# A hybrid decoder step on one core: sample readouts moved among the z tiles, gate squares summed on VectorE before one ones product, low parts of z and output weights made by adding DMAs

## The chip, the core and the metric

The kernel runs on one core of one Trainium2 chip. The core has a matrix engine (TensorE, "PE" in the profile, with "PEld" for its weight loads), a vector engine (VectorE, "DVE"), a scalar engine (ScalarE, "ACT"), GpSimd ("POOL") and SyncE ("SP"). Each engine runs its own instructions in order, and waits for others by semaphores. Here SP issues nearly all plain loads and stores, and POOL issues the DMAs that add into their destination. The metric is the device time of one execution in microseconds; the median of several runs counts.

## What is computed

One step of a decoder trunk for 512 prompt positions and 8 sample tokens, 520 columns in all, with features on the 128 partitions. A SwiGLU feed-forward block is followed by a mixer (a pooling branch and a state-space branch with a gate) and a second feed-forward block. The change lies in the mixer:

```python
def _hybrid_mixer(h, ...):
    proj = h @ w_in
    u_pool, z, xbc, dt_raw = jnp.split(proj, ...)
    pool_out, new_pool = _pool_mix(u_pool, ...)
    xbc_act, new_conv = _causal_conv(xbc, ...)
    ...
    y, h_new = _ssd_scan(xs_h, dt, A, B, C, ssm_h0, chunk)
    y = y + d_skip[:, None] * xs_h
    y = y.reshape(b, T, SSD_DIM) * jax.nn.silu(z)
    yg = y.reshape(b, T, SSD_GROUPS, SSD_DIM // SSD_GROUPS)
    yg = yg * lax.rsqrt(jnp.mean(yg * yg, axis=-1, keepdims=True) + EPS)
    y = yg.reshape(b, T, SSD_DIM) * ssd_norm
    cat = jnp.concatenate([pool_out, y], axis=-1)
    return cat @ w_out, new_pool, new_conv, h_new
```

## The kernel before

**Products in three parts.** TensorE multiplies fp32r numbers. To keep fp32 precision, weights and activations are split into a high part (rounded to fp32r) and a low part (what is left). `mm3` issues high x high (L123), high x low (L126) and low x high (L127) into one PSUM bank. A weight unit is 128 x 1024 fp32, 512 KB. `load_unit` has SP load it into a half of a raw tile (two pairs, four halves), and `split` makes the parts: ScalarE copies the high part (L107), VectorE subtracts it from the raw weights to get the low part (L114). `split` can also make the low part in another way, which the feed-forward blocks use for half of their units: ScalarE writes the negated weights, rounded to fp32r, into the low tile (L110), and POOL issues a DMA that reads the weights from HBM and adds them to it (L111). High and low tiles have three buffers each (`whi`, `wlo`), which all units of the mixer go through in the order of their use: a unit's tiles come free when TensorE is done with the unit three places before it.

**The mixer's stages.** Two strings, `CONV_PLAN` and `GATE_PLAN`, and a third, `LAST_PLAN`, set the order in which the program is written; a scheduler then orders the instructions of each engine by its own model of time. In the strings, `b` and `x` are convolution tiles, `p` pooling tiles, `z0` to `z7` the eight gate tiles (`zproj`: one weight unit, two halves of 260 columns in two PSUM banks, then VectorE multiplies by the norm into `zs`, L1113). `A` and `B` are the two parts of a chunk of the state-space scan, four chunks by two groups: `ssd_a` makes the decay tile `ab` (loaded by SP from a scratch in HBM, L1048) and `ssd_b` multiplies on TensorE (`yo`, `pst`, `yd`, L1083 to L1089). `s2` is two of the 16 sample readouts: SP loads a row `cb` (three buffers) and a state tile `h` (four buffers), and VectorE makes four products with an accumulated sum each (L975). `G` is the gate of a group (`gate`: silu of `zs`, product with X, L1139), and `H` its norm (`gate_out`). `o`, `g` and `h` are the 12 output weight units, four each of the pooling part and the two gate groups (`wout`: TensorE, then VectorE adds to the residual `h`, L1123). `n` fills the second feed-forward block's first products.

**The norm of a gate group** (`gate_out`, called by `H0` and `H1`). ScalarE squares four tiles of 128 x 520 (L1145). `rstd` sums them over the partitions with a product by a 128 x 128 tile of ones in plain fp32, four tiles accumulated into one bank, for each of the two halves (L170, tile `psr_y`): eight products for a group. ScalarE takes the root (L171), VectorE the reciprocal (L172), multiplies `zs` by it (L1152), ScalarE writes the high part `catg` (L1153), VectorE the low one (L1154), and the units `g` or `h` read them.

**PSUM.** The mixer has eight banks in rotation; a product's bank is the one used eight allocations earlier, and is free when that one has been read.

Of the kernel before, what the change touches and what calls it, by code (L numbers as in the profile page):

```python
# [12 lines left out]
ALU = mybir.AluOpType  # L13
# [4 lines left out]
D = 1024  # L18
# [21 lines left out]
    "c3 X1 m2 A3 B2 e0"  # L40
)
GATE_PLAN = (
    "A4 z0 B3 z1 m3 z2 B4 z3 s2 A5 z4 s2 B5 A6 z5 s2 s2 G0 z6 A7 z7 B6 s2 o0 H0 s2 o1 B7 s2 o2 s2 G1 "
    "o3 g0 g1 H1 g2 g3"
)
LAST_PLAN = "h0 h2 h1 n0 h3 n1 n2 n3"
# [15 lines left out]
def tile_trunk_step(ctx: ExitStack, tc: tile.TileContext, ins: dict, outs: dict):  # L62
    nc = tc.nc
# [6 lines left out]
    wp = ctx.enter_context(tc.tile_pool(name="wp", bufs=3, side="right"))  # L70
# [25 lines left out]
    def raw_tile(name):  # L96
        if not half:
            t = raw_pair(name)
            half.extend([t[:, 1], t[:, 0]])
        return half.pop()  # L100

    def split(src, n, name, hp, nb, tags, late=None):
        hi, lo = (hp.tile([P, 1024], F32R, tag=t, bufs=nb, name=f"{t}_{name}")[:, :n] for t in tags)
        h, l = hi, lo
        if len(src.shape) == 3:
            h, l = (t.rearrange("p (j c) -> p j c", j=src.shape[1]) for t in (hi, lo))
        nc.scalar.copy(h, src)  # L107
        q = 0 if late is None else n - late.shape[1]
        if late is not None:
            nc.scalar.activation(out=lo[:, q:], in_=src[:, q:], func=AF.Copy, scale=-1.0)  # L110
            nc.gpsimd.dma_start(out=lo[:, q:], in_=late, accum_op=ALU.add)  # L111
        if late is None or q:
            s = slice(0, q) if late is not None else slice(None)
            nc.vector.tensor_tensor(out=l[:, s], in0=src[:, s], in1=h[:, s].bitcast(F32), op=ALU.subtract)  # L114
        return hi, lo

    def load_unit(src, n, name):
        raw = raw_tile(name)[:, :n]
        nc.sync.dma_start(out=raw, in_=src)
        return split(raw, n, name, wp, 3, ("whi", "wlo"))  # L120

    def mm3(ps, whi, wlo, xhi, xlo, start, stop, pin=False, **kw):
        first = nc.tensor.matmul(ps, whi, xhi, start=start, stop=False, **kw)  # L123
# [84 lines left out]
    class Ffn:  # L208
# [310 lines left out]
        def down(self, c, lo, hi, after):  # L519
            n = hi - lo  # L520
            banks, units = {}, {}

            def part(d, ks):
                if d not in units:
                    units[d] = load_unit(ins[f"w{self.i}d"][d, :, lo * P : hi * P], n * P, f"{self.i}d{d}_{c}")
                    banks[d] = ps[0].tile([P, 2, 512], F32, tag="BE", bufs=2, name=f"dn{self.i}_{d}_{c}")
                wh, wl = units[d]
                for b in range(2):
                    for k in ks:
                        g = self.g[lo + k]  # L530
                        mm3(banks[d][:, b, :HB], ws(wh, k), ws(wl, k), g[:, 0, b], g[:, 1, b], k == 0, k == n - 1)

            def done(d):
                for b, hs in enumerate(HALVES):
                    nc.vector.tensor_tensor(out=h[:, d, hs], in0=banks[d][:, b, :HB], in1=h[:, d, hs], op=ALU.add)
                    after(d, b, hs)

            part(0, range(n - 1))
            part(1, range(n - 1))
            part(0, range(n - 1, n))  # L540
            done(0)
            part(1, range(n - 1, n))
            done(1)
            for d in range(2, KD):
                part(d, range(n))
                done(d)
# [54 lines left out]
    for j in range(KD // 2):  # L601
        for d in (j, j + KD // 2):
            q = slice(NVEC + d * NT if d else 0, NVEC + (d + 1) * NT)
# [87 lines left out]
    todo, late = [], []  # L691
# [48 lines left out]
def mixer(tc, ins, outs, e):  # L740
    nc = tc.nc
    cst, act, wp, tmp, dr, pool = (e[x] for x in ("cst", "act", "wp", "tmp", "dr", "pool"))
    ones = e["ones"]
    bank, load_unit, mm3, ws, v, rstd, rstds, vec, h, nx2, raw_tile, open_f2, fin, fill = (
        e[x] for x in ("bank", "load_unit", "mm3", "ws", "v", "rstd", "rstds", "vec", "h", "nx2", "raw_tile",
                       "open_f2", "fin", "fill"))
# [19 lines left out]
    X = mp.tile([P, NX, NT], F32, tag="X", name="X")  # L766
# [1 line left out]
    npp = mp.tile([P, 4, PAST], F32, tag="npp", name="npp")  # L768
    ncp = mp.tile([P, 12, 3], F32, tag="ncp", name="ncp")

    def inproj(src, name):
        wh, wl = load_unit(src, D, f"in{name}")
        bs = [bank(f"in{name}{b}") for b in range(2)]
        for b, hs in enumerate(HALVES):
            for k in range(KD):
                mm3(bs[b][:, :HB], ws(wh, k), ws(wl, k), xh[:, k, hs], xl[:, k, hs], k == 0, k == KD - 1)
        return bs
# [111 lines left out]
    def pooling(g):  # L889
        w = WINDOWS[g]  # L890
        bs = inproj(ins["w_in"][12 + g], f"p{g}")
        U = cv[0].tile([P, LP], F32, tag="cu", bufs=6, name=f"PU{g}")
        us = U[:, SAMPLE_P:LP].rearrange("p (b j) -> p b j", j=16)
# [214 lines left out]
    def zproj(j):  # L1108
        if not zbox:
            zbox.append(cv[0].tile([P, NX, NT], F32, tag="zs", name="zs"))  # L1110
        bs = inproj(ins["w_in"][16 + j], f"z{j}")
        for b, hs in enumerate(HALVES):
            nc.vector.tensor_tensor(out=zbox[0][:, j, hs], in0=bs[b][:, :HB], in1=r[:, hs], op=ALU.mult)  # L1113

    def wout(cat, j, d2, fin=None):
        wh, wl = load_unit(ins["w_out"][j, d2], 1024, f"wo{j}{d2}")
        for d in (2 * d2, 2 * d2 + 1):
            for b, hs in enumerate(HALVES):
                ps = bank(f"wo{j}_{d}{b}")
                for k in range(4):  # L1120
                    i = (d % 2) * 4 + k
                    mm3(ps[:, :HB], ws(wh, i), ws(wl, i), cat[:, 0, k, hs], cat[:, 1, k, hs], k == 0, k == 3)
                nc.vector.tensor_tensor(out=h[:, d, hs], in0=ps[:, :HB], in1=h[:, d, hs], op=ALU.add)  # L1123
                if fin is not None:
                    fin(d, b, hs)
# [15 lines left out]
    def gate_out(g):  # L1141
        zs = zbox[0]
        ry = mp.tile([P, NT], F32, tag="wph", name=f"yr{g}")
        for q in range(4):
            nc.scalar.activation(out=X[:, 4 * g + q], in_=zs[:, 4 * g + q], func=AF.Square)  # L1145
        for b, hs in enumerate(HALVES):
            rstd(ry, [X[:, 4 * g + q, hs] for q in range(4)], hs, 512, f"y{g}{b}")
        cat = cats[g] = xa.tile([P, 2, 4, NT], F32R, tag="xa", bufs=2, name=f"catg{g}")
        for q in range(4):
            i = 4 * g + q  # L1150
            gn = v("ssd_norm", i)
            nc.vector.tensor_tensor(out=zs[:, i], in0=zs[:, i], in1=ry, op=ALU.mult)  # L1152
            nc.scalar.activation(out=cat[:, 0, q], in_=zs[:, i], func=AF.Copy, scale=gn)  # L1153
            nc.vector.scalar_tensor_tensor(out=cat[:, 1, q], in0=zs[:, i], scalar=gn, in1=cat[:, 0, q].bitcast(F32),  # L1154
                                           op0=ALU.mult, op1=ALU.subtract)
# [13 lines left out]
    def outs_a():  # L1169
# [4 lines left out]

    stages = {
        "b": lambda j: conv(8 + j, inproj(ins["w_in"][j], f"bc{j}"), BC[:, j]),
        "x": lambda j: conv(j, inproj(ins["w_in"][4 + j], f"x{j}"), X[:, j]),
        "d": lambda j: box.update(dta=token_dt()) if j == 0 else (token_acs(box["dta"]), sample_decay()) if j == 1 else head_acs(),
# [7 lines left out]
        "A": lambda j: ssd_a(*ssd(j)),  # L1186
        "B": lambda j: ssd_b(*ssd(j)),
        "z": zproj,
        "o": lambda j: wout(catp, 0, j),
        "G": gate,  # L1190
        "H": gate_out,
        "g": lambda j: wout(cats[0], 1, j),
        "h": lambda j: wout(cats[1], 2, j, fin),
        "n": fill,
        "e": lambda j: outs_a(),
# [101 lines left out]
```

## Time and profile before

The median of three runs is 982.45 us. The execution that was profiled took 982.63 us, and its span on the core is 980.9 us, 1.7 us less. All times of the trace are microseconds from the start of that span.

| what | value |
|---|---|
| runs | 980.93, 982.45, 982.63 us |
| profiled execution, and its span | 982.63 us, 980.9 us |
| z tiles on TensorE | 472.9 to 532 us |
| output units on TensorE | 534.6 to 628 us |
| ScalarE busy from 445 to 605 us | 76.9 of 160 us |
| VectorE busy from 445 to 605 us | 141.5 of 160 us |
| GpSimd busy from 445 to 605 us | 37.1 of 160 us |

In the profile, a group's row gives its line, engine, operation, output and inputs, count, busy time, mean time of one, and the idle time of the engine just before it with what ended it. A window's row gives busy times by engine, the granted TensorE clock as a share of full speed, and the DMA engines' share.

### The profile page before, as it was taken

The numbers are of one execution on the slowest core, as the hardware profiler recorded it, in microseconds if no ns is written. First come the engines' busy times: TensorE is split into PE (matmuls) and PEld (weight loads), VectorE is DVE, ScalarE is ACT, GpSimd is POOL, SyncE is SP. The second block draws the span as 40 slices with busy tenths as digits, with TensorE's granted clock in tenths as the row PEclk, the third lists the DMA queues.
The fourth block names the chain that finished last, engine by engine and source line by source line (L and its number), as shares of the span: only waits on it lengthen the run. The fifth ranks groups of instructions, "written<-read, shape, count | busy, mean of one in ns | idle before, by whom it ended". The sixth has DMA issues, their size and how long they took to land.

```text
span 980.9 us, 20300 instructions
## 1 busy us (share of the span) xinstructions
PE 950.7 (97%) x7660; PEld 928.2 (95%) x7660; DVE 876.8 (89%) x1624; ACT 682.9 (70%) x1267; POOL 220.3 (22%) x321
## 2 busy tenths in 40 slices
PE   7999999999999999999999999999999999999996
PEld 6999999999999999999899998899999999999995
DVE  7999899989988698688979987999999998999976
ACT  8777777777777565694754335678888888887864
POOL 0111211221121000167311000113343233233300
PEclk9999999999999999999999999999999999999998
DMA  7666766576566242363334333357687768767732
GB/s 244 179 145 141 184 141 161 128 183 165 120 158 162 78 159 87 103 210 92 120 98 164 100 110 94 106 149 165 165 215 184 183 157 223 191 155 190 190 91 88
DMA packets 63858, 146.51 MB, mean 149 GB/s; under 512 B 9288, under 2 KB 22536, under 8 KB 63760
## 3 DMA queue, kind: packets, MB, share of 16 engines
q1 hardware_dynamic: 41168, 103.78, 33.3%
q0 software_dynamic: 22592, 41.43, 23.3%
q8 instruction: 60, 0.98, 0.4%
q14 instruction: 38, 0.31, 0.1%
HBM read 137.85 MB, written 7.34 MB: 148 GB/s over the span
## 4 chain that ended last, share of the span: by engine, by line
PE 82%; DVE 9%; ACT 3%; DMA 3%; issue 2%; SPq 0%; POOL 0%; DVEq 0%; ACTq 0%
PE A L127 7%; PE A L123 7%; PE A L126 7%; PE BE L123 6%; PE BE L126 6%; PE BE L127 6%; PE P L315 3%; PE wo L123 2%; PE wo L127 2%; PE wo L126 2%; PE inz L123 2%; PE inz L126 2%; PE inz L127 2%; PE A2d L126 2%; PE A2d L127 2%
## 5 line engine op out<-in xcount | busy, mean ns | idle before, releaser
L437 ACT COPY ac<-A 128x260 f32<-128x260 f32 x123 | 45.3, 370 | 19.5 <-PE A L127 19.2
L385 DVE TENSOR_TENSOR s<-raw 128x1024 f32<-128x1024 f32 x41 | 49.9, 1217 | 2.0 <-DMA raw<-in_w2gu 0.9
L107 ACT CAST whi_wo<-raw_wo 128x1024 fp32r<-128x1024 f32 x12 | 12.6, 1046 | 36.8 <-issue 10.3
L1005 POOL DMA_DIRECT2D out_nss<-hs x32 | 20.8, 649 | 76.8 <-DVE hs L1023 76.8
L126 PE MATMUL wo<-catg,whi_wo 128*128 128x260 f32 x128 | 36.4, 285 | 1.3 <-DVE catg L1154 1.3
L123 PE MATMUL wo<-catg,whi_wo 128*128 128x260 f32 x128 | 37.3, 292 | 0.3 <-DVE h L1123 0.3
L123 PE MATMUL inz<-xh_mx,whi_inz 128*128 128x260 f32 x128 | 37.5, 293 | 0.0
L315 PE MATMUL P<-xg_f,raw 128*128 128x260 f32 x128 | 31.7, 401 | 5.5 <-ACT sq_f L163 5.5
L126 PE MATMUL inz<-xl_mx,whi_inz 128*128 128x260 f32 x128 | 36.9, 288 | 0.0
L127 PE MATMUL inz<-xh_mx,wlo_inz 128*128 128x260 f32 x128 | 36.9, 288 | 0.0
L123 PE MATMUL inx<-xh_mx,whi_inx 128*128 128x260 f32 x128 | 36.4, 285 | 0.0
L127 PE MATMUL wo<-catg,wlo_wo 128*128 128x260 f32 x128 | 36.4, 285 | 0.0
L127 PE MATMUL inx<-xh_mx,wlo_inx 128*128 128x260 f32 x128 | 36.2, 283 | 0.0
L126 PE MATMUL inx<-xl_mx,whi_inx 128*128 128x260 f32 x128 | 36.1, 282 | 0.0
L315 PEld LDWEIGHTS P<-xg_f,raw 128*128 128x128 f32 x128 | 25.2, 201 | 9.3 <-ACT xg_f L192 5.5
L449 DVE TENSOR_TENSOR tg<-BE,ac 128x520 f32<-128x520 f32 x41 | 28.4, 693 | 5.5 <-PE BE L127 5.5
L869 DVE SCALAR_TENSOR_TENSOR A<-U,h,A 128x544 f32<-128x544 f32 x36 | 29.0, 805 | 4.0 <-ACT A L867 3.2
L458 DVE TENSOR_TENSOR tg<-tg,r_f 128x520 f32<-128x520 f32 x41 | 28.4, 694 | 1.2 <-ACT tg L456 1.0
L455 DVE TENSOR_TENSOR tg<-tg,r_f 128x520 f32<-128x520 f32 x41 | 28.4, 693 | 0.1
L386 DVE TENSOR_TENSOR s<-s,raw 128x512 f32<-128x512 f32 x41 | 28.0, 683 | 0.0
L387 DVE TENSOR_TENSOR s<-s,raw 128x512 f32<-128x512 f32 x41 | 28.0, 682 | 0.0
L456 ACT ACTIVATE tg<-tg 128x520 f32<-128x520 f32 x41 | 26.1, 638 | 2.5 <-DVE tg L455 2.2
(1798 smaller groups left out, 4788.2 us busy)
## 6 DMA issues: line engine op xcount, KB each, us to landing
raw<-in_w2gu SPq DMA_DIRECT2D x44, 512.0 KB, 4.9
raw<-in_w1gu SPq DMA_DIRECT2D x42, 512.0 KB, 4.7
raw_1d<-in_w1d SPq DMA_DIRECT2D x24, 384.0 KB, 4.0
raw_2d<-in_w2d SPq DMA_DIRECT2D x24, 384.0 KB, 4.2
raw_wo<-in_w_out SPq DMA_DIRECT2D x12, 512.0 KB, 4.3
ab<-scr_acs SPq DMA_DIRECT2D x8, 512.0 KB, 4.1
h<-in_state_ssm SPq DMA_DIRECT2D x16, 256.0 KB, 3.7
raw_inz<-in_w_in SPq DMA_DIRECT2D x8, 512.0 KB, 3.9
```

Source lines behind the costliest of these rows:

```text
L123: first = nc.tensor.matmul(ps, whi, xhi, start=start, stop=False, **kw)
L126: nc.tensor.matmul(ps, whi, xlo, start=False, stop=False, **kw)
L127: nc.tensor.matmul(ps, wlo, xhi, start=False, stop=stop, **kw)
L315: nc.tensor.matmul(self.banks[f, u][b][:, :HB], ws(self.raw[f][:, u], j + 4 * q), xg[:, slot[q]], start=j == q == 0, stop=j == 3 and q == ...
L385: nc.vector.tensor_tensor(out=s1, in0=diag, in1=up0, op=ALU.add)
L386: nc.vector.tensor_tensor(out=s2[:, 0], in0=s1[:, 1], in1=raw[:, 0, :nb], op=ALU.add)
L387: nc.vector.tensor_tensor(out=s2[:, 1], in0=s2[:, 0], in1=raw[:, 0, nb : 2 * nb], op=ALU.add)
L437: nc.scalar.copy(keep, out[:, :HB])
L449: nc.vector.tensor_tensor(out=tg, in0=self.BE[k][:, :, :HB], in1=a, op=ALU.add)
L455: nc.vector.tensor_tensor(out=tg, in0=tg, in1=r, op=ALU.mult)
L458: nc.vector.tensor_tensor(out=tg, in0=tg, in1=r, op=ALU.mult)
L869: nc.vector.scalar_tensor_tensor(out=A[:, :n], in0=U[:, j : j + n], scalar=w(j), in1=A[:, :n], op0=ALU.mult, op1=ALU.add)
```

## The change

Four edits. `load_unit` and `inproj` get a flag `late`, set for the z tiles and for the 12 output units: their low parts are made by ScalarE's negated copy and POOL's adding DMA, 20 units in all, and no longer by VectorE. In `gate_out` VectorE adds the squares of tiles 1 to 3 to those of tile 0, and the ones product is made of the sum alone, two products for a group. In `GATE_PLAN` the eight `s2` now stand after z0, z1, z2, z3, z4, G0, A7 and z7; before, they stood after z3, z4, z5 (twice), B6, H0, B7 and o2.

```diff
 GATE_PLAN = (
-    "A4 z0 B3 z1 m3 z2 B4 z3 s2 A5 z4 s2 B5 A6 z5 s2 s2 G0 z6 A7 z7 B6 s2 o0 H0 s2 o1 B7 s2 o2 s2 G1 "
+    "A4 z0 s2 B3 z1 s2 m3 z2 s2 B4 z3 s2 A5 z4 s2 B5 A6 z5 G0 s2 z6 A7 s2 z7 s2 B6 o0 H0 o1 B7 o2 G1 "
     "o3 g0 g1 H1 g2 g3"
 )
...
-    def load_unit(src, n, name):
+    def load_unit(src, n, name, late=False):
         raw = raw_tile(name)[:, :n]
         nc.sync.dma_start(out=raw, in_=src)
-        return split(raw, n, name, wp, 3, ("whi", "wlo"))
+        return split(raw, n, name, wp, 3, ("whi", "wlo"), src if late else None)
...
-    def inproj(src, name):
-        wh, wl = load_unit(src, D, f"in{name}")
+    def inproj(src, name, late=False):
+        wh, wl = load_unit(src, D, f"in{name}", late)
...
-        bs = inproj(ins["w_in"][16 + j], f"z{j}")
+        bs = inproj(ins["w_in"][16 + j], f"z{j}", True)
...
-        wh, wl = load_unit(ins["w_out"][j, d2], 1024, f"wo{j}{d2}")
+        wh, wl = load_unit(ins["w_out"][j, d2], 1024, f"wo{j}{d2}", True)
...
         for q in range(4):
             nc.scalar.activation(out=X[:, 4 * g + q], in_=zs[:, 4 * g + q], func=AF.Square)
+            if q:
+                nc.vector.tensor_tensor(out=X[:, 4 * g], in0=X[:, 4 * g], in1=X[:, 4 * g + q], op=ALU.add)
         for b, hs in enumerate(HALVES):
-            rstd(ry, [X[:, 4 * g + q, hs] for q in range(4)], hs, 512, f"y{g}{b}")
+            rstd(ry, [X[:, 4 * g, hs]], hs, 512, f"y{g}{b}")
```

The scheduler's order changes with it. On VectorE, around the first z tile, the rows after the state update of X stood so before (`U_6065` is the last convolution tile, read out of two PSUM banks; `ab_6111` and `ab_6180` are decay tiles of two scan parts):

```order
L1103 TENSOR_SCALAR X<-X,h,E_5779 128x128 x4
L1065 TENSOR_SCALAR ab_6111<-ab_6111,tok 128x128 x2
L781 TENSOR_TENSOR U_6065<-inx_6015,r_mx 128x260
L1065 TENSOR_SCALAR ab_6111<-ab_6111,tok 128x128 x2
L1065 TENSOR_SCALAR ab_6180<-ab_6180,tok 128x128 x4
L782 TENSOR_TENSOR U_6065<-inx_6016,r_mx 128x252
L783 TENSOR_TENSOR U_6065<-inx_6016,r_mx 128x8
L912 TENSOR_SCALAR PW_8_5943<-PW_8_5943,PU_5931 128x497
L912 TENSOR_SCALAR PW_8_5943<-PW_8_5943,PU_5931 128x8
L1070 TENSOR_TENSOR xdt_6131<-px_6106,tok 128x512
```

and stand so now:

```order
L1103 TENSOR_SCALAR X<-X,h,E_5779 128x128 x4
L1065 TENSOR_SCALAR ab_6111<-ab_6111,tok 128x128 x4
L781 TENSOR_TENSOR U_6065<-inx_6015,r_mx 128x260
L782 TENSOR_TENSOR U_6065<-inx_6016,r_mx 128x252
L783 TENSOR_TENSOR U_6065<-inx_6016,r_mx 128x8
L1065 TENSOR_SCALAR ab_6180<-ab_6180,tok 128x128 x4
L1070 TENSOR_TENSOR xdt_6131<-px_6106,tok 128x512
L912 TENSOR_SCALAR PW_8_5943<-PW_8_5943,PU_5931 128x497
L912 TENSOR_SCALAR PW_8_5943<-PW_8_5943,PU_5931 128x8
```

The readout of the convolution tile (L781 to L783) now stands ahead of the four instructions on `ab_6180`, and `xdt` ahead of the pooling tile.

On POOL, in the z stage, these rows stood before (`we` and `xw` are small factors and the weighted inputs of a scan part, `hst` the running state):

```order
L1073 TENSOR_TENSOR xw_6133<-xdt_6131,we_6113 128x512
L1052 TENSOR_TENSOR we_6513<-ab_6511,tok 128x8
L1095 TENSOR_TENSOR hst<-hst,cd_6119 128x512
L1073 TENSOR_TENSOR xw_6197<-xdt_6195,we_6182 128x512
L1052 TENSOR_TENSOR we_6648<-ab_6646,tok 128x8
L1073 TENSOR_TENSOR xw_6533<-xdt_6531,we_6513 128x512
```

and now (the DMAs are those of z3 to z6):

```order
L1073 TENSOR_TENSOR xw_6133<-xdt_6131,we_6113 128x512
L1052 TENSOR_TENSOR we_6565<-ab_6563,tok 128x8
L1095 TENSOR_TENSOR hst<-hst,cd_6119 128x512
L111 DMA wlo_inz_6479<-in_w_in 128x1024
L1073 TENSOR_TENSOR xw_6197<-xdt_6195,we_6182 128x512
L1052 TENSOR_TENSOR we_6701<-ab_6699,tok 128x8
L111 DMA wlo_inz_6591<-in_w_in 128x1024
L111 DMA wlo_inz_6726<-in_w_in 128x1024
L1073 TENSOR_TENSOR xw_6585<-xdt_6583,we_6565 128x512
L111 DMA wlo_inz_6814<-in_w_in 128x1024
```

The adding DMAs stand between the scan's own instructions, each behind the one before it.

On ScalarE, around the second group's norm, the rows stood so before (`whi_wo` are high parts of output units):

```order
L1145 ACTIVATE X<-zs 128x520 x4
L171 ACTIVATE yr_7451<-psr_y_7456,eps 128x260
L171 ACTIVATE yr_7451<-psr_y_7463,eps 128x260
L107 COPY whi_wo_7693<-raw_wo_7626 128x1024
L1153 ACTIVATE catg_7470<-zs,h 128x520 x3
L107 COPY whi_wo_7767<-raw_wo_7765 128x1024
L1153 ACTIVATE catg_7470<-zs,h 128x520
```

and now, with the squares further up (the first two pairs of copies are those of units g3 and h0, the third that of h2):

```order
L107 COPY whi_wo_7555<-raw_wo_7491 128x1024
L110 ACTIVATE wlo_wo_7556<-raw_wo_7491 128x1024
L107 COPY whi_wo_7638<-raw_wo_7636 128x1024
L110 ACTIVATE wlo_wo_7639<-raw_wo_7636 128x1024
L171 ACTIVATE yr_7462<-psr_y_7470,eps 128x260
L171 ACTIVATE yr_7462<-psr_y_7474,eps 128x260
L107 COPY whi_wo_7704<-raw_wo_7636 128x1024
L110 ACTIVATE wlo_wo_7705<-raw_wo_7636 128x1024
L1155 ACTIVATE catg_7478<-zs,h 128x520 x4
```

The squares of the second group stood behind the copies of g2, g3 and h0; they now stand ahead of them, and the root behind them. TensorE's order of tiles is otherwise the same, but for the ones products: the second group's, which were spread between matmuls of a g unit, now stand together at the end of unit g1.

## The prediction

> **What bounds the kernel now.** I read the page first: its busy times and the chain that ended last.
>
> ```profile
> span 980.9 us, 20300 instructions
> ...
> PE 950.7 (97%) x7660; PEld 928.2 (95%) x7660; DVE 876.8 (89%) x1624; ACT 682.9 (70%) x1267; POOL 220.3 (22%) x321
> ...
> PE 82%; DVE 9%; ACT 3%; DMA 3%; issue 2%; SPq 0%; POOL 0%; DVEq 0%; ACTq 0%
> ```
>
> TensorE is the bound: busy for 97% of the span and 82% of the chain. So the change can save in two ways only: by TensorE work that goes, and by waits of TensorE that go. VectorE's time is worth nothing by itself. Next, who made TensorE wait in the changed stage (460 to 640 us): the view of waits, with total, count and longest.
>
> ```profile
> PE psr_y L170 <- ACT X L1145: 1.6, 1, 1.6
> PE A L123 <- ACT ac L437: 1.4, 3, 0.5
> PE wo L126 <- DVE catg L1154: 1.3, 2, 0.6
> PE pb L1038 <- DVE U L783: 1.2, 1, 1.2
> PE px L1046 <- DVE xdt L1070: 0.7, 1, 0.7
> PE wo L123 <- DVE h L1123: 0.3, 1, 0.3
> ```
>
> The second row belongs to the feed-forward block behind, which the change leaves alone. The other five, 5.1 us, are the most that shorter waits can bring, with one exception, which the windows of 2 us around 470 show (busy times by engine, granted clock, DMA share, GB/s):
>
> ```profile
> 470.00:472.00 2.00, 0.52 (x3) 0.36 (x3) 2.00 (x9) 2.00 (x5) 1.30 (x6) 1.00 0.00 0
> 472.00:474.00 2.00, 1.61 (x10) 1.38 (x11) 2.00 (x4) 2.00 (x6) 2.00 (x2) 0.89 0.45 110
> 474.00:476.00 2.00, 2.00 (x11) 2.00 (x11) 2.00 (x6) 1.77 (x5) 0.97 (x1) 0.50 0.72 234
> 476.00:478.00 2.00, 2.00 (x15) 2.00 (x15) 2.00 (x8) 0.42 (x2) 0.39 (x1) 0.76 0.01 2
> ```
>
> Right behind the two waits at 471 us the granted clock falls to half. What it costs is 2 x (0.11 + 0.50 + 0.24) = 1.7 us.
>
> **Term 1: ones products.** From the chain of waits (start, duration):
>
> ```profile
> 461.62 6.42 DMA ab<-scr_acs
> ...
> 482.24 1.02 PE yd L1089 x16
> ...
> 535.71 0.12 PE wo L126
> ...
> 540.64 3.51 PE psr_y L170 x16
> ...
> 583.44 0.49 ACT yr L171
> ```
>
> Eight products are 16 recorded passes in 3.51 us, 0.22 each, all on the chain. A group keeps 4 passes of 16, so two groups lose 24 x 0.22 = **5.3 us**. The adds that replace them are six on VectorE (0.69 each by the product L1139 of the same shape, below), 4.1 us beside TensorE's work on z5 to g1. This is the surest term.
>
> **Term 2: the second group's squares.** They stood in ScalarE's queue behind the copies for g2, g3 and h0, and the last of these waits for g1 to free its tiles; so TensorE, done with g1, waited 1.6 us (first row of waits). The squares now stand ahead of these three, and the adds fall among the residual adds of o3 and g0, some 8 us before TensorE asks. I take the whole **1.6 us**; the bounds are 0 (another tile is late) and 1.6.
>
> **Term 3: the wait ahead of z0.** VectorE and TensorE in order of time:
>
> ```profile
> 467.90 2.70 DVE L1065 TENSOR_SCALAR ab<-ab,tok 128x128 f32<-128x128 f32 x6
> ...
> 470.85 0.16 DVE L783 TENSOR_TENSOR U<-inx,r_mx 128x8 f32<-128x8 f32 x1
> ...
> 471.61 0.68 DVE L1070 TENSOR_TENSOR xdt<-px,tok 128x512 f32<-128x512 f32 x1
> ```
>
> ```profile
> 468.85 1.09 PE L1089 MATMUL yd<-ab,xdt 128*64 128x128 f32 x16
> 471.15 0.30 PE L1038 MATMUL pb<-ident,BC 128*128 128x128 f32 x1 [1.21 <-DVE U L783]
> ...
> 472.34 0.55 PE L1046 MATMUL px<-ident,X 128*128 128x128 f32 x3 [0.67 <-DVE xdt L1070]
> ```
>
> `pb` wants the bank that the readout L783 frees, and that stood behind four instructions on a decay tile which landed only at 461.62 + 6.42 = 468.04. In the new order L783 stands ahead of them, and two low parts of z (1.35 each, below) are gone before it: the 1.2 us go. `px` still waits for `xdt`, which is behind that tile. The tile's load now has two z loads before it on SP's queue where it had one, and z1's adding DMA beside it, so it lands as now or up to 2 us later (an estimate). Four such instructions take 4/6 of 2.70 = 1.8 us or half of that, `xdt` 0.7. So `px` is ready between 469.6 and 472.5, and TensorE asks at 470.5: a wait of 0 to 2.0, of which I take 0.9. With the idle stretch under half of the present one, I count the clock as kept: 1.2 + 0.7 + 1.7 - 0.9 = **2.7 us**, bounds 1.6 and 3.6.
>
> The Trainium skill ("TensorE: Matmul & The Clock Gate", section "What's actually happening") says that the gate looks at free-running windows of about 3.4 us and closes after an idle one. The length agrees with the rows (1.7 us lost at half speed are 3.4 us), the idle time does not: 1.9 us were enough. By its rule the place of a wait in the window decides, so what is left of this wait could still close the gate; then term 3 is 1.0.
>
> **Term 4: the second group's output tiles.** Groups of instructions from 445 to 605 us, and that stretch's window:
>
> ```profile
> L114 DVE TENSOR_TENSOR wlo_wo<-raw_wo,whi_wo 128x1024 fp32r<-128x1024 f32 x12 | 14.6, 1218 | 0.6 <-ACT whi_wo L107 0.5
> ...
> L107 ACT CAST whi_wo<-raw_wo 128x1024 fp32r<-128x1024 f32 x12 | 12.6, 1046 | 36.8 <-issue 10.3 <-PE wo L126 8.9 <-PE inz L126 8.2
> L114 DVE TENSOR_TENSOR wlo_inz<-raw_inz,whi_inz 128x1024 fp32r<-128x1024 f32 x8 | 10.8, 1352 | 0.5 <-ACT whi_inz L107 0.5
> ...
> L1139 DVE TENSOR_TENSOR zs<-X,zs 128x520 f32<-128x520 f32 x8 | 5.2, 687 | 0.0
> ```
>
> ```profile
> 445.00:605.00 160.00, 154.94 (x1244) 145.77 (x1243) 141.54 (x361) 76.94 (x127) 37.10 (x43) 0.99 0.34 112
> ```
>
> VectorE loses 14.6 + 10.8 = 25.4 us of 141.5. Its rows of the norm:
>
> ```profile
> 583.95 1.78 DVE L172 RECIPROCAL yr<-yr 128x260 f32<-128x260 f32 x1 [3.37 <-ACT yr L171]
> ...
> 585.93 1.76 DVE L172 RECIPROCAL yr<-yr 128x260 f32<-128x260 f32 x1
> ...
> 589.36 2.52 DVE L1152 TENSOR_TENSOR zs<-zs,yr 128x520 f32<-128x520 f32 x4
> ...
> 596.29 0.75 DVE L1154 SCALAR_TENSOR_TENSOR catg<-zs,h,catg 128x520 fp32r<-128x520 f32 x1
> ```
>
> Let T be the end of g1. The root waits for h0's two copies: T + 2.1. One root 0.5, two reciprocals 3.5, two residual adds 0.8, four products 2.5: T + 9.4. ScalarE has h2's copies until g2's end, T + 0.9 + 5.8 (48 matmuls of 0.12), plus 2.1 = T + 8.8, then four high parts of about 0.7; the last low part is there at T + 13 to T + 14. TensorE wants the first tile at T + 0.9 + 11.6 = T + 12.5 and the fourth 1.1 later. Near enough that I take half of the 1.6 us (catg 1.3, h 0.3) as saved: **0.8**, bounds 0 and 1.6.
>
> **Term 5: the low parts.** ScalarE gets 20 negated copies of 1.05, 21 us on 76.9 of 160. POOL gets 20 issues on 37.1. The trace has the same operation at the same size, twice:
>
> ```profile
> L324 ACT ACTIVATE pwlo<-raw x2: 1052/1053/1054, 18.9 to 20.8; 128x1024 fp32r<-128x1024 f32 x2
> L325 POOL DMA_DIRECT2D pwlo<-in_w1gu x2: 848/920/991, 20.3 to 22.1; - x2
> ...
> DMA to landing us min/median/max: 5.6/6.2/6.8
> ```
>
> ```profile
> wlo_15b<-in_w2gu POOLq DMA_DIRECT2D x1, 256.0 KB, 9.0
> ```
>
> A low part is there 1.05 + 1.05 + 6.2 = 8.3 us after its tiles come free, that is after the unit three places before. Two units lie between, 2 x 5.8 = 11.6 us where nothing else does (g and h), more among the z tiles. Slack 3.3; with the slowest adding DMA of the trace (9.0) still 0.5. So **0**, hidden behind two units; uncovered, it would be what exceeds 11.6. Behind POOL's DMAs queue `xw` and `hst`; each DMA waits for copies that ScalarE does as soon as a unit frees its tiles, well before the next scan part.
>
> **Term 6: a new wait.** TensorE comes 1.9 + 1.7 us sooner to the first `yd` behind z0 (482.24), whose decay tile was ready thus:
>
> ```profile
> 477.93 1.21 DVE L1074 TENSOR_TENSOR ab<-ab,scm 128x1024 f32<-128x1024 f32 x1
> ```
>
> Ready at 479.1, slack 3.1 us against 3.6. VectorE has dropped three low parts before it, but ScalarE has got z2's negated copy: 0 to 0.5 + 1.0 = 1.5 us. I take **0.5** lost.
>
> The moved readouts cost no term: VectorE does the same 64 products, in z time where it has room.
>
> **Sum.** 5.3 + 1.6 + 2.7 + 0.8 - 0.5 = 9.9 us. The profiled execution took 982.6 (span 980.9 plus 1.7), 0.2 above the median: 982.6 - 9.9 - 0.1 = **972.6 us**. Its own range, all terms at their ends: 970.3 to 975.4. Behind it the second feed-forward block is paced by TensorE, so what is won should reach the end.
>
> **Rivals.**
> - *The clock falls all the same* at a wait that remains: 972.6 + 1.7 = 974.3. For it: 1.9 us sufficed at 471. Against it: the 1.6 us at 577 did not. Chance 0.10.
> - *Only TensorE's own work pays*: the waits come back at the next late tile, since VectorE still has some 120 us of work in 160 and ScalarE is busier. 982.5 - 5.3 = 977.2. Chance 0.10.
> - *The readouts hold VectorE.* Its queue is in order; a readout whose row `cb` (three buffers, one SP queue) has not landed stops the scan's instructions behind it. Some four `yd` waits of 1.2 us, the largest that VectorE caused, and one fall of the clock: 972.6 + 4.8 + 1.7 = 979.1. Against it: the first three rows land long before. Chance 0.12.
> - *Slower: low parts land late.* All 512 KB are read again and added in the destination, beside loads that share the DMA engines. From landings of 9.5 us on, three buffers no longer cover it: a unit then takes (2.1 + landing + 5.8) / 3. At 13 us that is 7.0, 1.2 more for each of 12 output units: 972.6 + 14 = 987. Against it: no adding DMA of the trace took over 9.0. Chance 0.10.
>
> The forecast has 0.58. A change under 0.2% (2 us) could not be told from none. Faster: 0.58 + 0.10 + 0.09 and parts of the last two, 0.85; same 0.05; slower 0.10. The range of 8 in 10, **969.5 to 979.5**, takes in all but the slower case and the tails.
>
> **What would show it.** Eight ones passes in all, in about 1.8 us; no wait of `psr_y` on L1145; `pb` with no wait, `px` at most 2 us, and a granted clock of 1.00 from 468 to 480; the waits for `catg` halved; adding DMAs of about 6 us and no matmul L127 waiting on one. A `wo` or `inz` matmul that waits for a DMA, or `yd` for L975's queue, would make it wrong.

## The result, and the profile after

The changed kernel takes 977.56 us (median of 22 runs, 973.32 to 982.96) beside 982.61 us of the kernel before (22 runs, 980.89 to 985.72). The ratio is 0.9947, with a 95% interval of 0.9934 to 0.9961. It is faster by 5.05 us, where 9.9 were forecast. The runs of the changed kernel lie twice as far apart as those of before: eight of the 22 took 973.3 to 975.0 us, at most 2.4 above the forecast of 972.6, and the slowest took as long as the kernel before. The execution that was profiled took 977.54 us.

The first lines of the page, and the shares of the chain that ended last:

```profile
span 975.8 us, 20309 instructions
...
PE 945.4 (97%) x7636; PEld 924.0 (95%) x7636; DVE 856.6 (88%) x1610; ACT 700.3 (72%) x1287; POOL 233.6 (24%) x341
...
PE 81%; DVE 7%; ACT 4%; DMA 4%; issue 2%; POOL 1%; SPq 0%; DVEq 0%; ACTq 0%; POOLq 0%
```

TensorE has 24 recorded passes fewer (7636 for 7660) and is still the bound. VectorE is relieved by 20 us, and its share of the chain fell from 9% to 7%; ScalarE and the DMAs have taken that up (3% each before, 4% now). Who made TensorE wait from 425 to 625 us (total, count, longest):

```profile
PE px L1046 <- ACT X L871: 2.3, 1, 2.3
PE px L1046 <- DVE xdt L1070: 1.2, 1, 1.2
PE inz L123 <- DVE E L1099: 1.0, 1, 1.0
PE pm L126 <- DVE catp L916: 0.6, 1, 0.6
```

The waits of `psr_y`, `catg`, `h` and `pb` are gone. The largest wait is a new one: in the middle of z1 the last transpose `px` waits 2.3 us for the silu of the last convolution tile (L871), and behind it the clock halves. Windows of 2 us (busy times of TensorE, its weight loads, VectorE, ScalarE, GpSimd; clock, DMA share, GB/s):

```profile
474.00:476.00 2.00, 2.00 (x19) 2.00 (x19) 1.84 (x5) 2.00 (x6) 1.21 (x2) 1.00 0.97 165
...
488.00:490.00 2.00, 1.41 (x8) 1.41 (x9) 1.32 (x7) 1.97 (x4) 0.00 (x0) 0.73 0.98 289
490.00:492.00 2.00, 2.00 (x11) 2.00 (x11) 2.00 (x9) 1.98 (x5) 0.00 (x0) 0.50 1.03 248
492.00:494.00 2.00, 2.00 (x18) 2.00 (x16) 1.45 (x10) 1.87 (x3) 1.24 (x2) 0.92 0.74 145
```

At 474 us, where the clock had been at 0.50, it is whole now. The fall has moved to 488 us and costs 2 x (0.27 + 0.50 + 0.08) = 1.7 us there, as much as before.

Why the silu is late is read from the chain of waits (start, duration):

```profile
473.50 6.02 DMA ab<-scr_acs
479.66 2.32 POOL we L1052
482.01 0.21 ACT we L1053
...
483.42 0.69 ACT ab L1063 x2
484.11 0.94 ACT whi_inz L107
485.06 0.96 ACT wlo_inz L110
486.02 0.58 ACT ab L1063 x2
486.61 1.28 ACT L871
487.91 0.64 ACT X L871
488.59 0.33 PE px L1046
```

The second decay tile lands 6.0 us after its issue. What GpSimd and ScalarE make of it (`we`, then L1058 and L1063), as well as z3's two copies, stands ahead of the silu in ScalarE's queue. Three things are longer than before: the tile is there 3.0 us later (479.5 for 476.6), GpSimd's `we` takes 2.32 us where it took 0.39, and z3 has a second copy of 1.0 us. Why `we` is slow here is not known. The groups of DMA issues from 445 to 535 us (count, KB each, median us from issue to landing) show that other loads are late too; before:

```profile
ab<-scr_acs SPq DMA_DIRECT2D x4, 512.0 KB, 4.1
...
cb<-scr_bc SPq DMA_DIRECT2D x8, 64.0 KB, 3.2
```

and after:

```profile
wlo_inz<-in_w_in POOLq DMA_DIRECT2D x8, 512.0 KB, 8.0
...
ab<-scr_acs SPq DMA_DIRECT2D x4, 512.0 KB, 6.0
...
cb<-scr_bc SPq DMA_DIRECT2D x13, 64.0 KB, 6.6
```

The decay tiles and the readouts' rows land 1.9 and 3.4 us later, beside adding DMAs of 8.0 us. VectorE pays for the rows: of the waits of VectorE from 445 to 580 us in the changed kernel, the one for a row is not in the list of before at all:

```profile
DVE junk L975 <- DMA cb<-scr_bc: 7.3, 4, 3.8
```

The Trainium skill ("DMA: Bandwidth & Descriptors", section "Issuing engines are not separate DMA queues") says that transfers issued by SP, ScalarE and GpSimd run on the same 16 engines and interleave. The rows agree: loads that SP issues became slower when GpSimd's were added. The plan moved the loads of the rows at the same time; the kernel without z's adding DMAs, below, tells the two apart.

### The profile page after: what moved, and what is told of

Its sections match the earlier page's. It is cut to its first block, busy times and chain, and to the rows that moved or that the text cites. A ratio compares the mean times of both kernels' runs of the same rounds, so it can differ in the third digit from the quotient of the medians.

```text
span 975.8 us, 20309 instructions
## 1 busy us (share of the span) xinstructions
PE 945.4 (97%) x7636; PEld 924.0 (95%) x7636; DVE 856.6 (88%) x1610; ACT 700.3 (72%) x1287; POOL 233.6 (24%) x341
## 4 chain that ended last, share of the span: by engine, by line
PE 81%; DVE 7%; ACT 4%; DMA 4%; issue 2%; POOL 1%; SPq 0%; DVEq 0%; ACTq 0%; POOLq 0%
PE A L127 7%; PE A L123 7%; PE A L126 7%; PE BE L123 6%; PE BE L126 6%; PE BE L127 6%; PE P L315 3%; PE wo L123 2%; PE wo L127 2%; PE wo L126 2%; PE A1d L127 2%; PE A1d L126 2%; PE A1d L123 2%; DMA ab<-scr_acs 1%; PE A2d L127 1%
## 5 line engine op out<-in xcount | busy, mean ns | idle before, releaser
L1123 DVE TENSOR_TENSOR h<-wo,h 128x260 f32<-128x260 f32 x48 | 19.4, 419 | 13.7 <-PE wo L127 13.7
L975 DVE SCALAR_TENSOR_TENSOR junk<-h,cb 128x128 f32<-128x128 f32 x64 | 21.5, 335 | 8.2 <-DMA cb<-scr_bc 7.3
L386 DVE TENSOR_TENSOR s<-s,raw 128x512 f32<-128x512 f32 x41 | 28.0, 682 | 0.0
```

Source lines behind the costliest of these rows:

```text
L386: nc.vector.tensor_tensor(out=s2[:, 0], in0=s1[:, 1], in1=raw[:, 0, :nb], op=ALU.add)
L975: nc.vector.scalar_tensor_tensor(out=junk, in0=h0[:, q], scalar=1.0, in1=cb, op0=ALU.mult, op1=ALU.mult, accum_out=ysm[:, 4 * g + q, b : b ...
```

## Experiments

Eight combinations of the three edits come first: S (squares summed), L (low parts by adding DMAs), P (the plan). Four kernels were then made to find the cost of L, one run repeats the change, and one kernel tries to do better. Each ratio is to runs of the kernel before taken beside it; each trace is of one execution.

**S alone.**

```diff
+            if q:
+                nc.vector.tensor_tensor(out=X[:, 4 * g], in0=X[:, 4 * g], in1=X[:, 4 * g + q], op=ALU.add)
...
-            rstd(ry, [X[:, 4 * g + q, hs] for q in range(4)], hs, 512, f"y{g}{b}")
+            rstd(ry, [X[:, 4 * g, hs]], hs, 512, f"y{g}{b}")
```

> The kernel before with one edit: the squares of tiles 1 to 3 are added to those of tile 0, two ones products a group. Theory A (each edit is worth what its own place shows, and the new wait of px on the silu of the last convolution tile, with the fall of the clock behind it, took back 4.0 us of the change): here the squares still stand behind other work in the plan of before, and nothing around z0 and z1 moves, so eight ones passes fewer per half are the gain: -5.3 us, with 0 to 1.6 more if psr_y's wait on L1145 goes too: 976 to 977. No wait of px on L871. Rival B (only TensorE's own work pays, and what waits came or went nets to nothing): the same -5.3. Rival D (the norm is on the path by VectorE: the adds come late): the six adds, 4.1 us, show as a wait of psr_y or catg, and the gain is under 2 us.

Measured: 988.78 us, 1.0060 of before (1.0045 to 1.0075): slower. The first row of TensorE's waits:

```profile
PE psr_y L170 <- DVE X L1147: 10.0, 2, 6.9
```

Rival D holds in full: TensorE waits 10 us for the adds in the two groups, and the clock falls behind both waits (5.1 us lost there).

**L alone** (the flag `late` for both kinds of units; shown is the one line of `load_unit`, the others are as in the change).

```diff
-        return split(raw, n, name, wp, 3, ("whi", "wlo"))
+        return split(raw, n, name, wp, 3, ("whi", "wlo"), src if late else None)
```

> The kernel before with one edit: the low parts of the z tiles and of the output units come from ScalarE's negated copy and the adding DMA. Theory A: this edit brings the new wait: the load of the decay tile of the chunk beside z1 lands at about 6 us in place of 3.9, z3's two copies stand ahead of the silu, so px waits for L871 by 1.5 to 3 us and the clock is at 0.5 for some 3.4 us behind it; the waits for catg go (1.6). Net slower than before by 0 to 4 us: 982 to 987, since the plan of before leaves the waits of pb and px ahead of z0 in place. Rival B: no gain and no loss, within 1 us of before. Rival C (the order of the plan makes the wait, not the low parts): no wait of px on L871, faster by 1 to 2 us.

Measured: 986.38 us, 1.0039 (1.0026 to 1.0051). The time is in the range of theory A, the reason is not: `px` did not wait for L871. The wait is at `psr_y`, and its cause is a row of VectorE in order of time, 6 us idle for a readout's row, with the gate's product L1139 behind it:

```profile
PE psr_y L170 <- ACT X L1145: 4.4, 1, 4.4
```

```profile
575.56 0.29 DVE L975 SCALAR_TENSOR_TENSOR junk<-h,cb 128x128 f32<-128x128 f32 x1 [6.06 <-DMA cb<-scr_bc]
```

**P alone** (the string `GATE_PLAN` of the change, nothing else).

> The kernel before with one edit: the plan with the readouts among the z tiles. Theory R (in the kernel before, the second group's squares came late because readouts stood ahead of L1139 on VectorE until 575, not because of ScalarE's copies; the moved readouts free that place): psr_y's wait of 1.6 us goes, and what the readouts cost among the z tiles is at most one wait of 1 to 2 us: 979.5 to 982. Rival L (VectorE's time is freed by the low parts; the plan alone only moves work into stages where VectorE is as busy): psr_y's wait stays or an equal one comes with a fall of the clock among the z tiles: 982 to 985.

Measured: 978.57 us, 0.9955 (0.9941 to 0.9969). This one line brings 3.9 us, 0.9 more than theory R's best. All of TensorE's waits from 425 to 625 us:

```profile
PE pb L1038 <- DVE U L783: 1.0, 1, 1.0
PE pm L126 <- DVE catp L916: 0.8, 1, 0.8
PE px L1046 <- DVE xdt L1070: 0.7, 1, 0.7
```

The waits for the squares (1.6) and for `catg` and `h` (1.6) are gone without any low part moved. The kernel before shows why, in VectorE's rows in order of time:

```profile
574.13 0.29 DVE L975 SCALAR_TENSOR_TENSOR junk<-h,cb 128x128 f32<-128x128 f32 x1
...
575.35 0.64 DVE L1137 SCALAR_TENSOR_TENSOR X<-X,h,ysm 128x8 f32<-128x8 f32 x4
575.92 0.69 DVE L1139 TENSOR_TENSOR zs<-X,zs 128x520 f32<-128x520 f32 x1
...
576.87 1.90 DVE L1139 TENSOR_TENSOR zs<-X,zs 128x520 f32<-128x520 f32 x3
```

The last readouts ran until 574.4, what is made of them until 576, and the four products that the squares read ended at 578.8. ScalarE began the four squares at 576.8, right behind the first of these products, and ended them at 579.4, 0.7 behind the last (a square takes about that long):

```profile
576.84 2.60 ACT L1145 ACTIVATE X<-zs 128x520 f32<-128x520 f32 x4
```

So ScalarE's copies were not what held the squares.

**S and P.**

> The kernel before with two edits: squares summed on VectorE, and the plan; low parts as before. With the squares alone psr_y waited 10.0 us for the adds (3.2 in the first group, 6.9 in the second). Theory R: with the readouts gone from o1 to o2 these waits fall to under 1 us together, and the kernel has 5.3 + 1.6 us less: 975 to 977, as fast as the whole change. Rival L (the adds need the time that the low parts give back): psr_y still waits 3 us or more, with a fall of the clock: 980 to 986.

Measured: 981.59 us, 0.9992 (0.9982 to 1.0003). Rival L holds:

```profile
PE psr_y L170 <- DVE X L1147: 5.3, 1, 5.3
```

VectorE runs behind here: the last readouts end at 569.3 (574.4 before; in the change they are done before 549), and low parts of 1.2 us each stand among the gate's products and the adds. Which of the two weighs more was not separated. The adds end so (VectorE in order of time), and TensorE had asked at 573.3:

```profile
575.11 0.69 DVE L1147 TENSOR_TENSOR X<-X 128x520 f32<-128x520 f32 x1
...
576.06 1.21 DVE L114 TENSOR_TENSOR wlo_wo<-raw_wo,whi_wo 128x1024 fp32r<-128x1024 f32 x1
577.19 1.43 DVE L1147 TENSOR_TENSOR X<-X 128x520 f32<-128x520 f32 x2
```

In the change the last add ends at 568.2 and TensorE asks at 576.4, 8 us of slack, as the prediction had it:

```profile
565.24 0.69 DVE L1147 TENSOR_TENSOR X<-X 128x520 f32<-128x520 f32 x1
...
567.47 0.69 DVE L1147 TENSOR_TENSOR X<-X 128x520 f32<-128x520 f32 x1
```

```profile
576.42 1.04 PE L170 MATMUL psr_y<-X,ones 128*128 128x260 f32 x4
```

**S and L, with the plan of before.**

> The change with the plan of before: squares summed and low parts by adding DMAs, readouts where they stood. Theory R: in the second group the readouts hold L1139 and the adds behind it, and the copies with their negations stand ahead of the squares on ScalarE: psr_y waits 4 to 8 us and the clock falls behind it: 983 to 989, slower than before. Rival L: the 25 us that VectorE no longer spends on low parts cover the adds; psr_y waits under 2 us: 976 to 979.

Measured: 982.85 us, 1.0003 (0.9994 to 1.0012). Theory R holds by its wait (`psr_y` 5.6 us on the adds), though the time lies just below the range that it gave.

**L and P, with eight products a group.**

> The change without the summed squares: eight products a group of ones again, plan and adding DMAs as in the change. If the effects add as in the change's own trace: the change plus the 24 passes of 0.22 us, 977.6 + 5.3 = 982 to 983.5, no wait of psr_y in either group. Rival (the squares' adds themselves cost something in the change, by VectorE): less than 5.3 us is lost, 979 to 981.5.

Measured: 982.79 us, 1.0006 (0.9988 to 1.0024), from 979.53 to 988.51: the effects add here, as far as so wide a spread lets one tell. With L and P in place the squares are worth 5.2 us, uncertain by about 2 by the two intervals.

The eight together. The waits are sums of the rows of TensorE's waits from 425 to 625 us, the time lost at half speed is 2 x the sum of (1 - clock) over windows of 2 us there, and the last column is the span less the waits, that loss, and 5.3 us where there are eight products a group:

| edits | median us | span | waits | half speed | remainder |
|---|---|---|---|---|---|
| none | 982.6 | 980.9 | 5.8 | 1.7 | 968.1 |
| S | 988.8 | 985.1 | 12.3 | 6.8 | 966.0 |
| L | 986.4 | 984.9 | 7.7 | 3.4 | 968.5 |
| P | 978.6 | 977.0 | 2.5 | 1.7 | 967.5 |
| S, P | 981.6 | 979.4 | 8.7 | 3.4 | 967.3 |
| S, L | 982.9 | 979.5 | 9.5 | 3.4 | 966.6 |
| L, P | 982.8 | 979.3 | 3.8 | 1.7 | 968.5 |
| S, L, P | 977.6 | 975.8 | 5.1 | 1.7 | 969.0 |

The summed squares lose 6.2 us alone and 3.0 beside P, and win 3.5 beside L and 5.2 beside both. The remainder stays within 3 us while the waits and the half speed together move by 15. So, to within 3 us, the time goes to TensorE's passes, its waits, and the falls of its clock. The spans are of single executions, up to 1.9 us faster than the median (S).

The plan alone brings 3.9 us, and all three edits 5.05; their intervals overlap. That the squares and the low parts together bring anything beside the plan is therefore not shown. Either of the two alone, added to the plan, loses 3 to 4 us.

**The change without z's adding DMAs** (`inproj` for the z tiles without the flag; the output units keep it).

> The change with one part undone: the low parts of the z tiles are again made by VectorE, those of the output units still by the adding DMA. Theory A: without z's copies and adding DMAs ScalarE has the silu early; no wait of px on L871 and no clock at half speed behind 488, while the wait of pb stays away by the new order: 973 to 975, 3 to 4 us faster than the change, with runs closer together. If VectorE's eight low parts (10.8 us) delay the readout L783 again, the wait ahead of z0 returns with its clock: 976 to 978. Rival B: as the change, 977 to 978. Rival C (the plan's order makes the wait): px still waits for L871 by about 2 us: 977 to 978.

Measured: 976.74 us, 0.9942 (0.9926 to 0.9959); not to be told from the change. Theory A is right on the spot (no wait of `px` on L871, no clock below whole from 425 to 625 us) and wrong on the sum: its 973 to 975 is missed, and its 976 to 978 asked for a fall of the clock that the profiled execution (975.48 us) does not have. TensorE's waits are still 4.8 us in all, 5.1 in the change; the larger ones are:

```profile
PE wo L123 <- DVE h L1123: 1.3, 2, 1.0
PE pm L126 <- DVE catp L916: 0.9, 1, 0.9
PE wo L123 <- DVE hst L1096: 0.7, 1, 0.7
PE px L1046 <- DVE xdt L1070: 0.7, 1, 0.7
PE pb L1038 <- DVE U L783: 0.6, 1, 0.6
```

The loads are on time again, with the plan of the change in place:

```profile
ab<-scr_acs SPq DMA_DIRECT2D x4, 512.0 KB, 4.4
...
cb<-scr_bc SPq DMA_DIRECT2D x10, 64.0 KB, 3.2
```

With the plan alone they take 4.7 and 3.2 us, with L alone 4.8 and 5.5. So the rows are late by z's adding DMAs; for the decay tiles the plan may have a small part.

**z3's split issued behind the silu.**

```diff
-        nc.scalar.activation(out=dst[:, SEQ:NT], in_=A[:, SEQ + 3 : SEQ + 3 + 4 * NS : 4], func=AF.Silu)
+        held["silu"] = nc.scalar.activation(out=dst[:, SEQ:NT], in_=A[:, SEQ + 3 : SEQ + 3 + 4 * NS : 4], func=AF.Silu)
...
-        bs = inproj(ins["w_in"][16 + j], f"z{j}", True)
+        with tc.issue_after(held["silu"].ins) if j == 3 else nullcontext():
+            bs = inproj(ins["w_in"][16 + j], f"z{j}", True)
```

> The change, but z3's split into parts is issued only behind the silu of the last convolution tile. Theory A with ScalarE's queue as the main cause: the two copies (2.1 us) are gone from ahead of L871, so px's wait shrinks from 2.3 us to under 0.5 and the clock stays: 973 to 975. Theory A with the late load of the decay tile as the main cause: L871 still comes behind the group that waits for that load; a wait of 0.5 to 1.5 us remains, and in some runs the clock's fall with it: 975 to 977. Rival: the wait has nothing to do with the span (what is won there is lost at the next late tile): 977 to 978.

Measured: 980.68 us, 0.9978 (0.9960 to 0.9996), above all three ranges and 3.1 us above the change. The wait at 488 us is gone, and one of the same length stands at 515 us, in TensorE's rows in order of time:

```profile
514.86 1.55 PE L1089 MATMUL yd<-ab,xdt 128*64 128x128 f32 x12 [2.23 <-DVE ab L1074]
```

VectorE was late there after 7.0 us in three waits for rows `cb` (2.4, 3.0 and 1.6 us, from 496 to 507 us). The clock fell behind this wait, and also at 474 us.

**The change again, another execution profiled.**

> The change, unchanged; another execution of it is profiled. Theory F (a wait of some 2 us drops the clock in some executions and not in others, which spreads the runs of the change from 973 to 983): the time of the profiled execution goes with the number of half-speed stretches before 960 us: none 973 to 975, one 976.5 to 979, two 980 to 983; the median stays at 977 to 978.5. Rival: the spread comes from landings of DMAs; the time does not go with that number.

Measured: 978.23 us, 0.9958 (0.9938 to 0.9978); the profiled execution took 978.56 us with one fall of the clock, at 474 us. Theory F gave 976.5 to 979 for one fall, and both executions fit. The granted clocks of all 34 runs of the change speak against it as the cause of the spread: 14 of them have the same mean clock, 0.995, and take from 972.9 to 981.2 us, where a thousandth of the clock is worth 1 us. Since TensorE lost 1.7 us at 474, it came later to `px` and waited 0.6 us there in place of 2.3. A new wait of 1.9 us stands in the first group, between the two halves of `psr_y`, and VectorE's rows show a readout's row as the cause again:

```profile
545.47 0.71 PE L170 MATMUL psr_y<-X,ones 128*128 128x260 f32 x2 [1.87 <-DVE E L1099]
```

```profile
544.51 0.29 DVE L975 SCALAR_TENSOR_TENSOR junk<-h,cb 128x128 f32<-128x128 f32 x1 [6.24 <-DMA cb<-scr_bc]
544.73 0.69 DVE L1099 TENSOR_TENSOR E<-yo,E 128x512 f32<-128x512 f32 x1
```

**Adding DMAs for z6 and z7 alone, and for z4 to z7** (the flag as `j >= 6` and `j >= 4`).

> The change with the adding DMA for the z tiles z6 and z7 and the output units alone; the low parts of z0 to z5 by VectorE. Theory Q (z's adding DMAs cost because they share the DMA engines with the scan's decay tiles and the readouts' rows, whose loads end by about 511 us): z6 and z7 come behind these loads, VectorE gets 2.4 us back ahead of the first output units, where the kernel without any adding DMA for z waits 0.7 and 1.0 us: 974.5 to 976.5, no wait of px on L871, no wait of VectorE for a row cb over 1 us. Rival (TensorE finds its next late tile anyway): as that kernel, 976 to 978.

> As the last, but with z4 to z7 by adding DMAs, z0 to z3 by VectorE. Theory Q: the DMAs of z4 and z5 run beside the last decay tile's load and the rows cb at 500 us, so these land 1 to 3 us later than with z6 and z7 alone, VectorE waits for a row, and some of the gain goes at a yd: 975.5 to 978, no wait of px on L871. Rival (only z0 to z3 and ScalarE's copies ahead of the silu matter, not the shared DMA engines): 973.5 to 975.5.

Measured: 978.11 us, 0.9955 (0.9938 to 0.9971), and 977.29 us, 0.9944 (0.9927 to 0.9960). Theory Q fails for the first: its range ended 1.6 us lower, VectorE waited 1.8 and 6.8 us for rows, and TensorE waited 2.6 us for VectorE's readout L1100 among the output units, which stands right behind the second of these waits (545 us). In the second VectorE waited 3.1 and 4.4 us for rows, as theory Q had it, but it is no slower than the first. The landings do go with the number of z's adding DMAs: with none, two, four and eight the rows take 3.2, 4.8, 6.1 and 6.6 us, the decay tiles 4.4, 4.5, 5.1 and 6.0. But this number does not move the median time by what could be told apart.

**z0 ahead of A4, low parts of z by VectorE.**

```diff
-    "A4 z0 s2 B3 z1 s2 m3 z2 s2 B4 z3 s2 A5 z4 s2 B5 A6 z5 G0 s2 z6 A7 s2 z7 s2 B6 o0 H0 o1 B7 o2 G1 "
+    "z0 A4 s2 B3 z1 s2 m3 z2 s2 B4 z3 s2 A5 z4 s2 B5 A6 z5 G0 s2 z6 A7 s2 z7 s2 B6 o0 H0 o1 B7 o2 G1 "
...
-        bs = inproj(ins["w_in"][16 + j], f"z{j}", True)
+        bs = inproj(ins["w_in"][16 + j], f"z{j}")
```

> The change with z's low parts by VectorE again, and in the plan z0 set ahead of the scan part A4 (z0 A4 s2 in place of A4 z0 s2), so that TensorE has 5.8 us of z0 in hand while VectorE comes to the readout L783 and to xdt. In the kernel with z's low parts by VectorE alone the two waits there were 0.6 and 0.7 us, in others up to 2.3 with a fall of the clock. Theory S (the span is 962 us, plus 5.3 for the ones products where there are eight a group, plus TensorE's waits from 425 us on, plus 1.7 for each half-speed stretch): px waits nothing, at most 0.6 us remain ahead of z0, no fall of the clock there: 974 to 976. Rival (what is saved there comes back as a wait at the next late tile): 976 to 978, with a new wait of 1 us or more behind z0 or among the output units.

Measured: 975.88 us (5 runs, 975.06 to 977.22), 0.9935 (0.9921 to 0.9949). It lies in theory S's range, with no fall of the clock from 425 to 625 us. The waits are not those of theory S: z0's first matmul waits 1.1 us for L783, and `px` waits for L871 again (1.5 us), as the rival had it. It is the fastest median of the study, but its interval overlaps that of the change.

## Why the prediction was right, and where it was not

The measured 977.56 us lies in the stated range, 969.5 to 979.5, by the room that the rivals were given, not by the sum. The sum's own range is added up wrongly: with all terms at their ends the gains are 12.1 and 5.4 us, which from 982.5 gives 970.4 to 977.1 us, not 970.3 to 975.4. The measured median lies just outside of that too. That the way and the range came true while half of the gain is missing is in part luck: terms 2 and 4 came for another reason than the one given or for one that is not shown. Of the signs that were named, eight passes, no wait on L1145 and no wait of `pb` came; the adding DMAs took 8.0 us and not about 6, and `px` waited 3.4 us in all, not at most 2.

**The bound, and term 1, held.** Eight passes stand where 32 stood, in two groups of 1.04 us; with L and P in place the time is 977.6 with them and 982.8 without. What the prediction did not say is that this term hangs on both other edits: with either of them missing, `psr_y` waits over 5 us for the adds.

**Term 2 (1.6 us) came whole, for another reason.** The prediction put the wait down to ScalarE's copies ahead of the squares. VectorE's readouts held the products that are squared; the plan alone removes the wait.

**Term 4 was forecast at half and came whole (1.6 us).** The plan alone removes these waits, but so do L alone and S alone (each with a longer wait of `psr_y` just ahead of them), so that the low parts which VectorE dropped are not shown to be the reason. "The moved readouts cost no term" was thus wrong on the good side: they are the part of the change that pays by itself, 3.9 us.

**Term 3 (2.7 us) came at 1.5 in one execution and not at all in the other.** `pb` no longer waits, but `px` and the first z matmul wait 2.1 us together (1.9 before) and 2.3 in the second execution. In the first the clock stayed whole there, in the second it fell as before. The wait of the first z matmul for VectorE's L1099 (1.0 us) is new, and the sum did not have it. `px` on `xdt` waited 1.2 us, between the bounds of 0 and 2.0.

**The step that failed is terms 5 and 6.** Term 5 asked only whether each low part would be ready in time. They were: in the change no z or output matmul waits for one. It counted 6.2 us to landing; those of z took 8.0 (median, up to 8.9) and those of the output units up to 9.6. It did not ask what eight DMAs of 512 KB do to the loads beside them; term 3 allowed for that in one load, and one rival named the shared engines, but only for the low parts themselves. The decay tiles took 6.0 us in place of 4.1, the rows `cb` 6.6 in place of 3.2. Term 6 looked for the new wait at one place, the first `yd` (0.5 us, at most 1.5), and found nothing for `px` on the silu. (It also counted TensorE 3.6 us early, though term 3 had left it a wait of 0.9, which makes it 2.7.) The first `yd` did not wait. In the first execution the wait on the silu cost 2.3 + 1.7 = 4.0 us; in the second, 0.6 us there and 1.9 at `psr_y`.

With the measured terms the first execution gives 5.3 + 1.6 + 1.5 + 1.6 - 4.0 = 6.0 us, against 5.1 between the two spans; 0.7 of the rest is a wait at 719 us in the feed-forward block that the trace of before does not have; the other 0.2 is not explained.

**The rivals.** The number is that of "only TensorE's own work pays" (977.2), and its mechanism was half there: waits did go, and others of nearly the same sum came (5.8 us before, 5.1 and 5.7 after). "The readouts hold VectorE" named one of the causes, a row that has not landed, and got a chance of 0.12 because the first three rows land early; the later ones do not. In the first execution these rows cost VectorE 7.3 us, but none of TensorE's waits from 425 to 625 us is put down to them; in the second one of them cost TensorE the 1.9 us at `psr_y`. Five kernels moved the spot of the loss, and none is shown to have removed it: undoing z's adding DMAs wholly (also with z0 moved ahead) or for some tiles, or taking z3's copies from ahead of the silu, brought no median that can be told below the change's.

What stays open: whether the loads are late by their share of the DMA engines or by their place among the packets was not separated, and a version with the rows `cb` loaded earlier was not tried, nor one with z's adding DMAs and without those of the output units. No execution of the change of 973 to 975 us was profiled, so what those eight runs did otherwise is not known.

## What to carry to other kernels

In this kernel the edit that took work off the bounding engine and gave it to another paid only where that other engine had been freed ahead of the place; do the edits singly and in pairs before crediting any of them. Here the shortest one, the order of eight readouts, brings nearly all of the gain by itself. For a transfer that replaces engine work, look not only at when it lands but at which loads run beside it and who waits for those. Where the waits of the bounding engine are 1 to 2 us each and several engines feed it, count on removed waits to come back in part at another tile: here 5.8 us of waits became 5.1 and 5.7.

## What was not expected of the hardware

The clock's fall is not a matter of the wait alone. Idle time of 1.6 us around 473 us in S with P, and of 2.1 us in the profiled change, left it whole. 1.5 us in S alone and 2.1 us in L with P halved it, and each of these half-speed stretches lost 1.7 us; behind the waits of 4.4 us and more, and once behind one of 2.2 us (at 515 us), the loss was 3.4 us. The Trainium skill ("TensorE: Matmul & The Clock Gate", section "What's actually happening") has free-running windows of some 3.4 us, so that the place of a wait in the window matters: the spread of outcomes and the steps of 1.7 us agree with that. Its condition of a whole idle window does not, since 1.5 us were enough.
